# Modulation loads on ScalarE's DMA queue, and two early row loads at the first change of stage

## The chip, the cores and the metric

The kernel runs on one core of a Trainium2 chip. The metric is device time in microseconds, the median of three runs: 1107.7, from 1103.93 to 1109.38. The core has a matrix engine PE, the vector engine DVE, the scalar engine ACT and the general engine POOL; SP computes nothing here and issues DMAs. Each engine works through its own instructions in order. A DMA is issued by an instruction of one engine, runs on the core's 16 DMA engines, and raises a semaphore when it has landed.

## What is computed

One step of a two-layer model on 128 prompt tokens and 256 latent tokens (384 in all), width 1024, in float32. Layer 0 mixes tokens by a gated delta rule (8 heads, two directions, chunks of 64), layer 1 by windowed attention; each layer ends in a gated feed-forward part of width 2816.

```python
def modulation(cvec, w_ada, b_ada):              # w_ada: 1024 x 6144 per layer
    m = (silu(cvec) @ w_ada + b_ada)[:, None, :]
    return split(m, 6)                           # shift, scale, gate, twice

for i in range(2):
    mp, ms = modulation(c_ctx, ...), modulation(c, ...)
    h = rmsnorm(x, g0) * (1 + m[1]) + m[0]       # per stream, prompt and latent
    y = delta_mixer(h) if i == 0 else attention(h)
    x = x + m[2] * rmsnorm(y, g1)
    h = rmsnorm(x, g2) * (1 + m[4]) + m[3]
    f = (silu(a) * b) @ w_down                   # a, b: depthwise conv of h @ w_up
    x = x + m[5] * rmsnorm(f, g3)

# delta_mixer: per head and chunk solve (I + strict_lower(beta k k^T * decay)) u = rhs,
# then a scan over chunks carries the state S
```

The modulation weights w_ada are 48 MB for the two layers and are read whole, though each is used for two vectors only.

## The kernel before, in words

**Stages.** The kernel runs through layer 0's mixer (DeltaNet), a first feed-forward stage, attention and a second feed-forward stage. Each large product is split into a high and a low part of both factors, so three matmuls stand for one; ACT makes the high part of a weight (`whi`), DVE the low part (`wlo`), both from a raw 0.5 MB buffer (`raw`, three of them) that SP's queue fills. A stage ends in `tm` (L857): the output product, then per block of 128 tokens the squares on ACT (`stat`), `y<-bank,gate` on DVE (`t_gated`, L706), the update of `x`, squares again, `y<-x,arow` (`t_scale`), and diag matmuls on PE (`t_quarter`) that transpose y for the next stage, where its high and low parts are made (`hhi`, `hlo`). The last three products of each output bank (`tail`) are held back, so that PE has work while the first block goes through this. I call this a change of stage. `gate` and `arow` are rows of the modulation, read from DRAM (`gdram`, `adram`) and broadcast to 128 partitions by `t_rows` (L662), 1 MB each. At the first change of stage `tm` calls `hook` (L1142), which waits until all heads are done, takes a pool `dn3` in the memory that they leave, and loads `x` again (`x_prompt` 0.5 MB, `x_sample` 1 MB), because the DeltaNet stage uses x's memory as scratch.

**The modulation.** `t_ada` (L514) loads w_ada in slabs of 1 MB (128 x 2048): 40 of them through the slots `ada`, which are two buffers (`ada0`, `ada1`), and further one-use buffers that `lend` (L388) adds when some memory is free, among them the 1 MB buffers (`mem`) of heads 4 to 7 (L1411). `back` (L359) returns a slab's buffer. `t_mod` (L523) multiplies the slabs with silu(c) on PE (`bank<-ada,sc`), in 12 chunks per layer; a table `FILL` holds some chunks for the changes of stage.

**The inverse.** `t_inverse` (L1439) takes a head's matrix N through DRAM: it stores N (`nd<-N`), reads diagonal 16 x 16 blocks back (`tmp<-nd`, `X<-nd`), inverts them on POOL, stores the inverse's blocks (`zd<-inv`) and reads them in another layout (`x<-zd`; for the first heads the target is a part of x's memory). I call these transfers legs.

**The order of the work.** A list scheduler, `Sched` (L101), writes each engine's instructions. Tasks are generators that ask for an engine by a letter (P, A, V, G, and Q for SP's queue), for an event or for slots; of all tasks that wait, the one that could start first by the planner's costs is placed. `Sched.dma` (L136) costs a DMA at `DQ` = 0.47 us on Q, and at its bytes over `DBW` = 360 GB/s on one clock that all DMAs share. `Net.dma` (L322) issues all of them from SP:

```python
self.nc.sync.dma_start(out=out, in_=src)
```

The planner's costs only set the order. On the chip an instruction starts when the one before it on its engine and the semaphores it waits for let it. The DMAs' landings raise one of eight semaphores (`DMAHW0` to `DMAHW7` in the order's rows), and an instruction that issues a DMA can wait for one of them too.

Of the kernel before, what the change touches and what calls it, by code (L numbers as in the profile page):

```python
# [11 lines left out]
F32 = mybir.dt.float32  # L12
# [5 lines left out]
D = 1024  # L18
# [4 lines left out]
H = 8  # L23
# [27 lines left out]
DL1 = 0.25  # L51
DL2 = 1.6
DMIN = 0.06
DBW = 360.0
DQ = 0.47
SV = 0.0
ZD = 1
# [18 lines left out]
class Event:  # L76


    def __init__(self):
        self.time, self.waiters = None, []  # L80
# [20 lines left out]
class Sched:  # L101
# [5 lines left out]
    def __init__(self):  # L107
        self.free = dict.fromkeys("PAVGQ", 0.0)
        self.pending, self.runnable = [], deque()
        self.eng, self.start, self.cost, self.acts, self.bw, self.seq = None, 0.0, 0.0, [], 0.0, 0  # L110
        self.work = {}


# [5 lines left out]
    def set(self, ev):  # L119
        self.acts.append(lambda end: self._set(ev, end))  # L120

    def put(self, slots, *items):
        for i in items:
            self.acts.append(lambda end, i=i: self._put(slots, i, end))

    def use(self, letter, cost):
        assert letter == self.eng, (letter, self.eng)
# [7 lines left out]

    def dma(self, nbytes):  # L136

        self.use("Q", DQ)
        beg = max(self.start + self.cost + DL1, self.bw)
        self.bw = beg + max(DMIN, nbytes / (DBW * 1e3))  # L140
        ev = Event()
        ev.time = self.bw + DL2
        return ev


# [119 lines left out]
class Net:  # L265
# [55 lines left out]

    def dma(self, out, src):  # L322
        ev = self.s.dma(4 * math.prod(out.shape))
        self.nc.sync.dma_start(out=out, in_=src)  # L324
        return ev

    def load(self, out, src):
# [31 lines left out]
    def back(self, slots, item):  # L359

        if not any(item is o for o in self.once):
            self.s.put(slots, item)

    def free_bank(self, bank):

# [148 lines left out]
    def t_ada(self):  # L514
        for l, n, half in self.msrc:
            raw = yield self.ada, 1
            yield "Q"
            self.s.put(self.adaful, (raw, self.dma(raw, self.i["w_ada"][l, n, half])))

    def mod_prio(self):  # L520
# [336 lines left out]
    def tm(self, act, ready, plan, l, w, tail, nxt, hook=None):  # L857


        uses = {}  # L860
        for pieces in plan:
            for k, _ in pieces:
                uses[k] = uses.get(k, 0) + 1
        full = {k: Event() for k in uses}
        self.s.spawn(self.t_act(act, ready, plan, uses, full), 3)
        left = {hf: sum(h == hf for t in plan for _, h in t) for hf in range(2)}
        grid = lambda n: [[Event() for _ in range(n)] for _ in range(3)]
        ctx = dict(nxt=nxt, rg=grid(2), sq=grid(2), y=grid(2), sq2=grid(2), xa=grid(2), diag=[Event() for _ in range(3)], ready=[Event() for _ in range(3)])
        total = dict(left)
        acc = {}  # L870

        def piece(b, k, hf, wt, j, first, last):
            hi, lo = wt
            ah, al = full[k].val
            t, c = slice(b * 128, (b + 1) * 128), HALF[j]
            o = acc[hf][b]
            self.mm(o, ah[:, t], hi[:, c], start=first, stop=False)
            self.mm(o, ah[:, t], lo[:, c], start=False, stop=False)
            self.mm(o, al[:, t], hi[:, c], start=False, stop=last)

        held = []
        for n, pieces in enumerate(plan):
            if n == (len(plan) - tail if hook else 0):
                pool = hook() if hook else self.pool
                if hook:
                    pool = yield from pool
                ctx["gate"] = pool.tile([128, 2, D], F32, name="gate"), Event()
                self.s.spawn(self.t_rows(self.gates[l, w], self.gdram[l][w], *ctx["gate"]), 3)
                if nxt is not None:
                    ctx["arow"] = pool.tile([128, 2, D], F32, name="arow"), Event()  # L890
                    ctx["diags"] = [pool.tile([128, 128], F32, name=f"diag{b}") for b in range(3)]
                    ctx["shift"] = [pool.tile([128, n], F32R, name=f"shift{n}{m}") for m, n in enumerate((128, 128, 16))], Event()
                    self.s.spawn(self.t_shift(self.AB[nxt], *ctx["shift"]), 3)
                    self.s.spawn(self.t_rows(self.AB[nxt], self.adram[nxt[0]][nxt[1]], *ctx["arow"]), 3)
            wt = yield self.wready, 1
            for k, _ in pieces:
                yield full[k]
            if n >= len(plan) - tail:
                held.append((wt, pieces))
                continue  # L900
            for j, (k, hf) in enumerate(pieces):
                if hf not in acc:
                    acc[hf] = yield (self.bk if hf == 0 else self.pj), 3
                for b in range(3):
                    yield "P"
                    piece(b, k, hf, wt, j, left[hf] == total[hf], left[hf] == 1)
                left[hf] -= 1
                uses[k] -= 1
                if not uses[k] and k < self.recycle:
                    self.s.put(self.ahs, full[k].val)  # L910
            self.s.put(self.ws, wt)
        base = dict(left)
        if nxt is not None:
            self.boundary = Event()
        for hf in range(2):
            if not left[hf]:
                for b in range(3):
                    self.t_acc(b, hf, acc[hf][b], ctx)
        evs = []
        for b in range(3):  # L920
            for hf in range(2):
                for wt, pieces in held:
                    for j, (k, h) in enumerate(pieces):
                        if h == hf:
                            yield "P"
                            piece(b, k, hf, wt, j, False, left[hf] == 1)
                            left[hf] -= 1
                    if b == 2 and hf == max(h for _, h in pieces):
                        self.back(self.ws, wt)
                if base[hf]:  # L930
                    left[hf] = base[hf]
                    self.t_acc(b, hf, acc[hf][b], ctx)
            evs.append(self.s.spawn(self.t_block(b, ctx), 1 + b * 0.1))
        if nxt is not None:
            self.nearly = NE
            self.s.spawn(self.fm_first(NE, [([r[g] for r in ctx["rg"]], range(4 * g, 4 * g + 4), slice(0, NTOK)) for g in range(2)]), 10)
            self.s.set(self.fill[2 * l + w])
            evs.append(self.filled[2 * l + w])
        for e in evs:
            yield e  # L940
        if nxt is not None:
            self.s.set(self.boundary)
            self.boundary = None
# [150 lines left out]
    def delta(self, pool, nxt):  # L1094
        tc, i, s = self.tc, self.i, self.s
        with ExitStack() as late:
# [4 lines left out]
            t = lambda n, shape, dt=F32: hp.tile(shape, dt, name=n)  # L1101
# [12 lines left out]
                   for n in range(NB)]  # L1114
# [5 lines left out]
                                     R=t("R", [128, 2, 128]), sn=t("sn", [128, 2, 128]))])  # L1120
            self.norms = Slots([dict(osb=t(f"osb{n}", [128, 3, 128]), **{k: t(f"{k}{n}", [128, 3]) for k in ("so", "rt", "rs")})
                                for n in range(2)])
            self.odone = odone = [[Event()] for _ in range(H)]
            self.gateh, self.written = set(), set()
            s.spawn(self.t_zero(nqs, works), 8)
# [16 lines left out]
            def hook():  # L1142
                for e in chains + [o[0] for o in odone]:
                    yield e
                inner.close()
                pp = late.enter_context(tc.tile_pool(name="dn3", bufs=1))
                self.t512 = Slots([pp.tile([128, 512], F32, name=f"y{n}") for n in range(6)])
                wlast = self.pair(pp, "d")
                self.once.append(wlast)
                s.put(self.wlast, wlast)  # L1150
                yield "Q"
                self.load_x()
                return pp

            self.ahs, self.recycle = Slots(self.hslices()), 0
            plan = [[(2 * j, hf), (2 * j + 1, hf)] for hf, j in DN_OUT]
            yield from self.tm(self.oact, odone, plan, 0, 0, min(TAIL, 3), nxt, hook)

    def columns(self, m):
# [97 lines left out]
    def t_chain(self, h, t):  # L1257
        V, A, s = self.V, self.A, self.s
# [27 lines left out]
        N, Q, Y = nq["N"], nq["Q"], nq["Y"]  # L1286
# [106 lines left out]
        e = yield "AV" if h not in self.gateh else "V"  # L1393
# [13 lines left out]
        yield xc0  # L1407
        if h < H - 4:
            s.put(self.hslots, t)
        else:  # L1410
            self.lend(t["mem"].rearrange("p (j c) -> p j c", j=4))  # L1411

# [556 lines left out]
```

## Time and profile before

| what | value |
|---|---|
| median of three runs | 1107.7 us |
| profiled execution | 1107.74 us |
| its span | 1106.0 us |
| PE busy | 1062.2 us (96%) |
| PEld busy | 927.4 us |
| DVE busy | 696.2 us |
| ACT busy | 549.8 us |
| POOL busy | 235.0 us |
| mean granted clock of TensorE | 0.985 |
| bytes of the DMA queue | 176.61 MB |

PEld is PE's weight load, which runs beside matmuls. The clock is a share of full speed, so 1.00 is 2.4 GHz throughout. The span begins with the first instruction of the profiled execution; every "at so many us" counts from there. Of the views shown below, windows give the busy time of each engine in a stretch with the number of its instructions; the chain of waits has the start of a step, its length, and what it ran through; a timeline has the start, the length, engine, line, operation, output<-inputs, how many, and in brackets how long the engine was idle before and what released it. "SPq" is an issue of a DMA on SP's queue: its length is the issue's, not the transfer's.

### The profile page before, as it was taken

To read this page: it belongs to the slowest core of one execution; us is meant where nothing else is said; L and a number is where in the kernel's file an instruction comes from. 1 tells how busy PE (TensorE), PEld (TensorE's weight loads), DVE (VectorE), ACT (ScalarE), POOL (GpSimd) and SP (SyncE) were. 2 spreads that over 40 slices of the span, in tenths; PEclk is the share of its full clock that TensorE was granted. 3 is DMA by queue.
4 is the path that set the end of the run, shared out by engine and by line. 5 is a ranking of instruction groups with operands and counts; after the bars stand their busy time and mean duration, and the time that the engine had idled before them with its cause. 6 is when DMAs were issued, how large, how long until landed. Compare 5 with 4: busy or idle time off the path is not lost.

```text
span 1106.0 us, 19683 instructions
## 1 busy us (share of the span) xinstructions
PE 1062.2 (96%) x7397; PEld 927.4 (84%) x7397; DVE 696.2 (63%) x1685; ACT 549.8 (50%) x1127; POOL 235.0 (21%) x403
## 2 busy tenths in 40 slices
PE   6999899999998999999999999999999999999997
PEld 4887778899785999999988869776769999999886
DVE  5578656988546565656654456878577556566434
ACT  4576754767534444444543345566455444445422
POOL 0023545646202122222200021000031222221000
PEclk9999999999899999999999999998999999999999
DMA  9768664356345534533583346621514434335431
GB/s 364 279 224 293 189 193 127 104 167 204 96 166 223 199 126 132 196 120 128 169 316 126 113 133 220 212 95 41 192 35 142 132 118 132 126 123 172 129 119 57
DMA packets 73567, 177.86 MB, mean 161 GB/s; under 512 B 25816, under 2 KB 38744, under 8 KB 66432
## 3 DMA queue, kind: packets, MB, share of 16 engines
q1 hardware_dynamic: 73472, 176.61, 47.7%
q8 instruction: 58, 0.95, 0.3%
q14 instruction: 37, 0.30, 0.1%
HBM read 169.45 MB, written 7.13 MB: 160 GB/s over the span
## 4 chain that ended last, share of the span: by engine, by line
PE 81%; DMA 6%; DVE 5%; POOL 4%; issue 2%; ACT 1%; SPq 1%; DVEq 0%; POOLq 0%; ACTq 0%
PE bank L299 79%; PE bank L319 2%; POOL tmp L261 1%; DMA tmp<-nd 1%; DVE y L261 1%; POOL inv L261 1%; DMA gate<-gdram 1%; DMA nd<-N 1%; DMA x<-zd 1%; DMA ada<-in_w_ada 1%; DVE x L261 1%; DMA first<-in_w_ada 1%; SPq L324 1%; POOL stat L261 1%; DVE hlo L261 1%
## 5 line engine op out<-in xcount | busy, mean ns | idle before, releaser
L299 PE MATMUL bank<-hhi,whi 128*128 128x384 f32 x832 | 283.8, 341 | 4.1 <-DVE vf L261 2.8
L299 PE MATMUL bank<-hlo,whi 128*128 128x384 f32 x832 | 283.6, 341 | 0.2 <-DVE hlo L261 0.2
L299 PE MATMUL bank<-hhi,wlo 128*128 128x384 f32 x832 | 282.2, 339 | 0.0
L261 DVE TENSOR_TENSOR wlo<-raw,whi 128x1024 fp32r<-128x1024 f32 x151 | 184.9, 1225 | 64.1 <-ACT whi L261 64.0
L261 DVE SCALAR_TENSOR_TENSOR u<-bank,cw_ff,u 128x127 f32<-128x127 f32 x352 | 122.3, 410 | 145.3 <-ACT u L261 145.3
L261 ACT ACTIVATE whi<-raw 128x1024 fp32r<-128x1024 f32 x151 | 158.6, 1052 | 58.3 <-PE bank L299 46.8
L299 PEld LDWEIGHTS bank<-hhi,whi 128*128 128x128 f32 x832 | 156.7, 188 | 14.6 <-DVE vf L261 3.4
L299 PEld LDWEIGHTS bank<-hlo,whi 128*128 128x128 f32 x832 | 156.7, 188 | 4.2 <-issue 2.0
L299 PEld LDWEIGHTS bank<-hhi,wlo 128*128 128x128 f32 x832 | 156.7, 188 | 1.2 <-issue 0.8
L261 ACT ACTIVATE u<-bank,cw_ff 128x384 f32<-128x384 f32 x88 | 59.2, 673 | 177.2 <-PE bank L299 177.2
L261 POOL TENSOR_TENSOR g<-u 128x384 f32<-128x384 f32 x44 | 79.6, 1809 | 307.0 <-DVE u L261 276.6
L299 PE MATMUL bank<-whi,hhi 128*128 128x512 f32 (+1 forms) x246 | 96.7, 393 | 0.0
L299 PE MATMUL bank<-wlo,hhi 128*128 128x512 f32 (+1 forms) x246 | 94.1, 383 | 0.0
L299 PE MATMUL bank<-whi,hlo 128*128 128x512 f32 (+1 forms) x246 | 94.0, 382 | 0.0
L261 POOL TENSOR_TENSOR stat<-stat,mhalf 128x1 f32<-128x1 f32 x24 | 15.7, 656 | 253.0 <-DVE stat L261 253.0
L299 PE MATMUL bank<-hhi,wlol 128*128 128x384 f32 x200 | 67.9, 339 | 0.0
L299 PE MATMUL bank<-hlo,whil 128*128 128x384 f32 x200 | 67.7, 339 | 0.0
L299 PE MATMUL bank<-hhi,whil 128*128 128x384 f32 x200 | 67.7, 339 | 0.0
L261 DVE TENSOR_TENSOR wlol<-raw,whil 128x1024 fp32r<-128x1024 f32 x38 | 46.3, 1218 | 14.0 <-ACT whil L261 14.0
L299 PEld LDWEIGHTS bank<-whi,hhi 128*128 128x128 f32 x246 | 46.6, 190 | 9.6 <-issue 0.7
L299 PEld LDWEIGHTS bank<-whi,hlo 128*128 128x128 f32 x246 | 46.7, 190 | 9.2
L299 PEld LDWEIGHTS bank<-wlo,hhi 128*128 128x128 f32 x246 | 46.8, 190 | 8.0
(253 smaller groups left out, 1740.0 us busy)
## 6 DMA issues: line engine op xcount, KB each, us to landing
raw<-in_ffn_w_up SPq DMA_DIRECT2D x88, 512.0 KB
ada<-in_w_ada SPq DMA_DIRECT2D x32, 1024.0 KB
raw<-in_ffn_w_down SPq DMA_DIRECT2D x44, 512.0 KB
raw<-in_dn_w_in SPq DMA_DIRECT2D x29, 512.0 KB
first<-in_w_ada SPq DMA_DIRECT2D x6, 1024.0 KB
head<-in_w_ada SPq DMA_DIRECT2D x4, 1024.0 KB
raw<-in_dn_w_out SPq DMA_DIRECT2D x8, 512.0 KB
gate<-gdram SPq DMA_DIRECT2D x4, 1024.0 KB
```

What stands on the lines that cost most here:

```text
L261: return f(out, *a, **k)
L299: self.nc.tensor.matmul(out, lhsT, rhs, **kw)
L319: self.nc.tensor.transpose(out, src, ident)
L324: self.nc.sync.dma_start(out=out, in_=src)
```

## The change

Three things are changed. The modulation slabs of `t_ada` are issued from ACT (`yield "A"`), and the planner has a bandwidth clock of its own for each of the two queues (360 and 250 GB/s); a slab's buffer counts as free 2.0 us after its last use in the planner (`ADAGO`). At the first change of stage the rows gate and arow no longer get tiles of the pool dn3: the 1 MB buffers of heads 4 and 5, which were lent to slabs, receive them as soon as those heads are done (`lentrows`). And `hook` lends two more 1 MB tiles of dn3 (`adb0`, `adb1`) to slabs, after x's loads.

```diff
-DBW = 360.0
+DBWS = dict(Q=360.0, A=250.0)
+ADAGO = 2.0
@@ class Sched
-    def put(self, slots, *items):
+    def put(self, slots, *items, lag=0.0):
         for i in items:
-            self.acts.append(lambda end, i=i: self._put(slots, i, end))
+            self.acts.append(lambda end, i=i: self._put(slots, i, end + lag))
@@ def dma(self, nbytes):
-        self.use("Q", DQ)
-        beg = max(self.start + self.cost + DL1, self.bw)
-        self.bw = beg + max(DMIN, nbytes / (DBW * 1e3))
+        e = self.eng
+        self.use(e, DQ)
+        beg = max(self.start + self.cost + DL1, self.bw[e])
+        self.bw[e] = beg + max(DMIN, nbytes / (DBWS[e] * 1e3))
...
@@ class Net
-        self.nc.sync.dma_start(out=out, in_=src)
+        dict(Q=self.nc.sync, A=self.nc.scalar)[self.s.eng].dma_start(out=out, in_=src)
@@ def back(self, slots, item):
-            self.s.put(slots, item)
+            self.s.put(slots, item, lag=ADAGO if slots is self.ada else 0.0)
@@ def t_ada(self):
-            yield "Q"
+            yield "A"
@@ def tm
-                ctx["gate"] = pool.tile([128, 2, D], F32, name="gate"), Event()
-                self.s.spawn(self.t_rows(self.gates[l, w], self.gdram[l][w], *ctx["gate"]), 3)
+                if hook:
+                    ctx["gate"], ctx["arow"] = self.lentrows
+                else:
+                    ctx["gate"] = pool.tile([128, 2, D], F32, name="gate"), Event()
+                    self.s.spawn(self.t_rows(self.gates[l, w], self.gdram[l][w], *ctx["gate"]), 3)
...
@@ def hook
                 self.load_x()
+                self.lend(*[pp.tile([128, 4, 512], F32, name=f"adb{n}") for n in range(2)])
@@ def t_chain
         if h < H - 4:
             s.put(self.hslots, t)
+        elif h < H - 2:
+            rows, ev = t["mem"].rearrange("p (s d) -> p s d", s=2), Event()
+            self.lentrows.append((rows, ev))
+            s.spawn(self.t_rows(*((self.gates[0, 0], self.gdram[0][0]), (self.AB[0, 1], self.adram[0][1]))[len(self.lentrows) - 1], rows, ev), 3)
         else:
             self.lend(t["mem"].rearrange("p (j c) -> p j c", j=4))
```

**First place: SP's queue at the first head's inverse.** `nd0<-N0` is the leg out, `tmp<-nd0` and `X<-nd0` the leg back. Before:

```order
L324 DMA ada0_93<-in_w_ada 128x2048
L324 DMA ada1_94<-in_w_ada 128x2048
L324 DMA raw2_76<-in_dn_w_in 128x1024
L324 DMA nd0_627<-N0_624 128x6x128
L324 DMA mdram0_128<-modev0_95 4x512 x2
L324 DMA dm0_592<-gcdram_547 128x768
L324 DMA nd1_632<-N1_629 128x6x128
L324 DMA ada0_93<-in_w_ada 128x2048
L324 DMA tmp_641<-nd0_627 24x16x16
L324 DMA X_639<-nd0_627 24x16x16
```

The same place in the changed kernel:

```order
L327 DMA zd2_638<-Y2_636 128x192
L327 DMA raw0_74<-in_dn_w_in 128x1024
L327 DMA nd0_627<-N0_624 128x6x128
L327 DMA raw1_75<-in_dn_w_in 128x1024
L327 DMA tmp_641<-nd0_627 24x16x16
L327 DMA X_639<-nd0_627 24x16x16
L327 DMA raw2_76<-in_dn_w_in 128x1024
```

The three slabs are gone from SP's queue there, and a weight stands between the two legs in their place.

**Second place: ACT in the DeltaNet stage.** `vf1` and `head` are parts of a head, `modev` a chunk of modulation. ACT issues six slabs in its first 102 rows; here, at the tiles of head 7, come the next two in the changed kernel:

```order
L264 ACTIVATE vf1_591<-bank0_63,cw_dn_154 128x384
L264 ACTIVATE whi1_79<-raw0_74 128x1024
L264 COPY modev1_96<-bank3_66 128x512
L264 ACTIVATE junk_83,ss2_606<-bank5_68 128x128 x3
L327 DMA ada0_93<-in_w_ada 128x2048
L327 DMA ada1_94<-in_w_ada 128x2048
L264 ACTIVATE bank1_64<-bank1_64 128x384
```

In the kernel before no DMA stands on ACT; in the changed one none stands between its rows 102 and 230, and these are 230 and 231.

**Third place: the first change of stage.** SP's queue before, with `head2` a lent head buffer that takes a slab:

```order
L324 DMA raw2_76<-in_ffn_w_up 128x1024
L324 DMA raw0_74<-in_ffn_w_up 128x1024
L324 DMA head2_581<-in_w_ada 128x2048
L324 DMA x_71<-in_x_prompt 128x1024
L324 DMA x_71<-in_x_sample 128x2x1024
L324 DMA gate_3869<-gdram00_134 128x2048
L324 DMA arow_3870<-adram01_131 128x2048
L324 DMA raw1_75<-in_ffn_w_up 128x1024
```

In the changed kernel gate and arow are read further up in SP's queue, into `head4` (row 115) and `head0` (row 154); x's loads are rows 160 and 161. ACT at this place in the changed kernel, with what each instruction waits for (`DMAHW5` and `DMAHW6` are raised here by the loads of x_prompt and x_sample; `junk,stat00` are the squares of block 0):

```order
L264 COPY modev1_96<-bank4_67 128x512 [waits DMAHW4_49,PE_49]
L264 ACTIVATE whi2_81<-raw2_76 128x1024 [waits DMAHW3_49]
L327 DMA ada0_93<-in_w_ada 128x2048 [waits DMAHW7_49,DMAHW5_49]
L327 DMA ada1_94<-in_w_ada 128x2048 [waits DMAHW2_49]
L327 DMA adb0_3864<-in_w_ada 128x2048 [waits DMAHW5_49]
L327 DMA adb1_3865<-in_w_ada 128x2048 [waits DMAHW6_49]
L264 ACTIVATE junk_83,stat00_84<-bank6_69 128x512 [waits DVE_49]
L264 ACTIVATE junk_83,stat00_84<-bank2_65 128x512 [waits PE_49,Activation_49]
```

And PE there in the changed kernel, at block 0's diag matmuls:

```order
L302 MATMUL bank7_70<-wlod_3852,hhi_72 128x512
L302 MATMUL bank7_70<-whid_3851,hlo_73 128x512
L302 MATMUL bank3_66<-diag0_3866,y0_3845 128x128 x4
L302 MATMUL bank4_67<-diag0_3866,y1_3846 128x128 x4
L302 MATMUL bank6_69<-shift162_3871,shift1280_3869 128x512
L302 MATMUL bank6_69<-shift162_3871,shift1281_3870 128x512
L302 MATMUL bank5_68<-shift162_3871,shift1280_3869 128x512
L302 MATMUL bank5_68<-shift162_3871,shift1281_3870 128x512
L302 MATMUL bank7_70<-whid_3851,hhi_72 128x512
```

Four slabs stand on ACT ahead of block 0's squares where there were none. On PE the last nine matmuls of the tail (the last row is the first of them) now stand behind diag0; in the kernel before the whole tail and one slab's product stand ahead of it.

## Rows read from the trace of the kernel before

**Rows 1.** Windows: busy us (count) of PE, PEld, DVE, ACT, POOL; clock, DMA, GB/s

```profile
80.00:126.00 46.00, 40.47 (x244) 33.09 (x242) 34.50 (x102) 32.73 (x69) 16.25 (x44) 1.00 0.84 269
126.00:175.00 49.00, 46.20 (x683) 37.01 (x684) 28.65 (x85) 25.10 (x71) 26.08 (x80) 0.93 0.57 178
260.00:292.00 32.00, 30.01 (x405) 26.77 (x407) 22.25 (x60) 19.40 (x50) 15.20 (x43) 0.99 0.54 151
355.00:500.00 145.00, 145.00 (x852) 140.06 (x853) 86.73 (x173) 64.88 (x87) 28.70 (x16) 1.00 0.45 151
```

**Rows 2.** The chain of waits, first heads: start us, length us, what.

```profile
85.07 8.46 DMA nd<-N
93.59 6.01 DMA tmp<-nd
...
117.97 8.39 DMA x<-zd
...
148.85 9.47 DMA ada<-in_w_ada
...
164.96 6.18 DMA tmp<-nd
```

**Rows 3.** The chain of waits, one of the last heads.

```profile
265.46 2.87 DMA nd<-N
268.35 2.40 DMA tmp<-nd
...
286.96 2.73 DMA x<-zd
```

**Rows 4.** Timeline of SP's queue, 62 to 163 us, slabs: first, last.

```profile
62.95 0.35 SPq L324 DMA_DIRECT2D ada<-in_w_ada  x1
...
161.63 1.28 SPq L324 DMA_DIRECT2D ada<-in_w_ada  x2
```

**Rows 5.** Timeline of DVE at the first head's third leg.

```profile
126.39 0.38 DVE L261 STREAM_TRANSPOSE x<-x 128x192 f32<-128x192 f32 x1 [3.92 <-DMA x<-zd]
```

**Rows 6.** Timeline of SP's queue at the first change of stage.

```profile
323.11 0.38 SPq L324 DMA_DIRECT2D head<-in_w_ada  x1
...
324.02 0.78 SPq L324 DMA_DIRECT2D x<-in_x_sample  x1
```

**Rows 7.** The chain of waits at the first change of stage.

```profile
324.90 12.48 DMA gate<-gdram
```

**Rows 8.** Timelines of ACT and of DVE at the first change of stage.

```profile
327.54 0.60 ACT L261 ACTIVATE junk<-bank 128x512 bf16<-128x512 f32 x1 [1.59 <-PE bank L299]
...
337.41 1.29 DVE L261 TENSOR_TENSOR y<-bank,gate 128x512 f32<-128x512 f32 x2 [7.57 <-DMA gate<-gdram]
338.62 1.40 DVE L261 SCALAR_TENSOR_TENSOR x<-y,stat,x 128x512 f32<-128x512 f32 x2
```

**Rows 9.** Timeline of PE at the first change of stage.

```profile
337.32 0.39 PE L299 MATMUL bank<-wlo,hhi 128*128 128x512 f32 x1
337.55 0.39 PE L299 MATMUL bank<-whi,hlo 128*128 128x512 f32 x1
338.16 1.06 PE L299 MATMUL bank<-ada,sc 128*32 128x512 f32 x8 [0.23 <-DVE y L261]
343.21 3.48 PE L299 MATMUL bank<-diag,y 128*128 128x128 f32 x16 [3.98 <-DVE diag L261]
...
354.83 2.05 PE L299 MATMUL bank<-diag,y 128*128 128x128 f32 x16 [0.67 <-DVE diag L261]
```

**Rows 10.** The tile ada, its loads: least/median/most ns to issue; waits.

```profile
L324 SPq DMA_DIRECT2D ada<-in_w_ada x32: 327/340/1122, 10.9 to 705.9; - x32
```

**Rows 11.** Page, part 5: the power of the squares' sums on POOL.

```profile
L261 POOL TENSOR_TENSOR stat<-stat,mhalf 128x1 f32<-128x1 f32 x24 | 15.7, 656 | 253.0 <-DVE stat L261 253.0
```

**Rows 12.** Timeline of PE at the third change of stage.

```profile
807.66 2.05 PE L299 MATMUL bank<-diag,y 128*128 128x128 f32 x16 [0.16 <-DVE diag L261]
...
821.17 2.05 PE L299 MATMUL bank<-diag,y 128*128 128x128 f32 x16 [1.91 <-DVE diag L261]
```

More of the change, by code (lines that the diff above doesn't have):

```diff
@@ L109, in __init__ @@
         self.pending, self.runnable = [], deque()
-        self.eng, self.start, self.cost, self.acts, self.bw, self.seq = None, 0.0, 0.0, [], 0.0, 0
+        self.eng, self.start, self.cost, self.acts, self.seq = None, 0.0, 0.0, [], 0
+        self.bw = dict(Q=0.0, A=0.0)
         self.work = {}
@@ L136, in dma @@
     def dma(self, nbytes):
-        self.use("Q", DQ)
-        beg = max(self.start + self.cost + DL1, self.bw)
-        self.bw = beg + max(DMIN, nbytes / (DBW * 1e3))
+        e = self.eng
+        self.use(e, DQ)
+        beg = max(self.start + self.cost + DL1, self.bw[e])
+        self.bw[e] = beg + max(DMIN, nbytes / (DBWS[e] * 1e3))
         ev = Event()
-        ev.time = self.bw + DL2
+        ev.time = self.bw[e] + DL2
         return ev
@@ L886, in tm @@
                     pool = yield from pool
-                ctx["gate"] = pool.tile([128, 2, D], F32, name="gate"), Event()
-                self.s.spawn(self.t_rows(self.gates[l, w], self.gdram[l][w], *ctx["gate"]), 3)
+                if hook:
[3 more added lines that the diff above has]
+                    self.s.spawn(self.t_rows(self.gates[l, w], self.gdram[l][w], *ctx["gate"]), 3)
+                if nxt is not None and not hook:
+                    ctx["arow"] = pool.tile([128, 2, D], F32, name="arow"), Event()
+                    self.s.spawn(self.t_rows(self.AB[nxt], self.adram[nxt[0]][nxt[1]], *ctx["arow"]), 3)
                 if nxt is not None:
-                    ctx["arow"] = pool.tile([128, 2, D], F32, name="arow"), Event()
                     ctx["diags"] = [pool.tile([128, 128], F32, name=f"diag{b}") for b in range(3)]
@@ L893, in tm @@
                     self.s.spawn(self.t_shift(self.AB[nxt], *ctx["shift"]), 3)
-                    self.s.spawn(self.t_rows(self.AB[nxt], self.adram[nxt[0]][nxt[1]], *ctx["arow"]), 3)
             wt = yield self.wready, 1
@@ L1122, in delta @@
                                 for n in range(2)])
+            self.lentrows = []
             self.odone = odone = [[Event()] for _ in range(H)]
```

## The prediction, made before the changed kernel had run

> **What bounds the kernel now.** I read the busy time by stage first, then the chain of waits, then the timelines of the DMA-issuing SP queue, of PE and of DVE at the places where PE stood still. The stages show one bound: PE. From 355 to 500 us, in the first feed-forward stage, PE is busy 145.00 of 145.00 us [rows 1], and nothing that moves a load can help there. PE stands still before that, in the DeltaNet stage: 5.53 us of 46 between 80 and 126 us, 2.80 of 49 between 126 and 175, with a granted clock of 0.93 in the latter [rows 1]. The chain of waits says why: in those two stretches it runs through transfers, not through arithmetic. The matrix N of a head goes out to DRAM in 8.46 us and comes back in part in 6.01; the inverse's blocks come back in 8.39; a modulation slab holds PE's order for 9.47, and a later return takes 6.18 [rows 2]. The same three legs take 2.87, 2.40 and 2.73 us for one of the last heads [rows 3]. What differs is what stands ahead of them in SP's queue: between 62 and 163 us twelve 1 MB modulation slabs are issued there, in three places two at once just ahead of a leg [rows 4]. DVE, in order, stands 3.92 us behind the third leg [rows 5].
>
> The other still place is the first change of stage. Gate and arow are issued there behind a slab, x and two weights [rows 6]; gate lands 12.48 us later [rows 7], and DVE waits 7.57 us for it [rows 8]. PE then idles 3.98 us before the first diag matmul [rows 9].
>
> **The change part by part, made against the profiled execution: 1107.74 us, its span 1106.0 and 1.74 around it; the median of the three runs, 1107.7, is the same number.**
>
> *Slabs leave SP's queue.* Forty loads go to ACT, and the planner, whose costs changed, also puts them at other places. In the new order SP holds no slab around the first head's legs, and ACT holds four between the first heads and head 7's tiles where SP held twelve; the next stands behind head 7. So 8 MB leave the crowded stretch and come back after 225 us. Legs at the quiet price would be shorter by 8.46 - 2.87, 6.01 - 2.40, 8.39 - 2.73 and 6.18 - 2.40, and the wait of 9.47 would go: 28.1 us of the chain. That is not the gain, because PE works beside most of it. What PE can take back is its idle time, 5.53 + 2.80 = 8.3 us, less what a quiet stretch with the same small matmuls leaves idle, 32.00 - 30.01 = 2.0 [rows 1]: 6.3. The clock of 0.93 over 49 us is 3.4 us of PE's work lost after idling (1.2 instead of 2.4 GHz for part of it); I take 1 of it. Together 7.3. From below: nothing or a loss, if the eight slabs' matmuls, which filled holes, now leave holes and later stand in the way. From above: all 8.3 idle and 3.4 of clock, 11.7.
>
> *ACT issues.* An issue holds its queue 0.34 us by the median of the slabs' row [rows 10]; 40 are 13.6 us on ACT, whose work in the feed-forward stage is 64.88 of 145 us [rows 1]. That cover hides all but those inside a change of stage, two of the second: 0.7 us. Dearer is that ACT waits in order. A load can wait for the buffer's last reader, which the planner's 2 us are for, and also for the landing of another DMA that used the same completion semaphore before; 8 semaphores serve both queues. Behind it stand the conversions of weights and the evictions on which PE waits. No row of before has such a wait on ACT. Bounds: below 0.7, since most waited-for transfers stand far ahead in the order; above, for the thirteen loads between 225 and 320 us, four that hold ACT for a quiet leg of 2.4 us each [rows 3], with half of the 10 us reaching PE: 5. I take 0.7, the row of the issue.
>
> *Gate and arow early.* They land long before use, so DVE's 7.57 us end. What is late next is ACT. Its order there now has four slab loads ahead of block 0's two squares, and the third and fourth wait on the semaphores that x_prompt's and x_sample's loads raise (order, third place). So the squares start when x_sample has landed, though block 0 does not need it. In before the line ahead of gate's landing was half a weight's MB, a slab, 1.5 MB of x and gate itself, 4 MB in 12.48 us: 3.1 us a MB [rows 7]. x_sample therefore landed about 334.3, gate's MB earlier; without the slab it would be 331.2, and with the two slabs that ACT issues just before, sharing the engines, 334.3 again. From there: 0.5 of issues, two squares of some 0.75 [rows 8], y 0.65, the power on POOL with its neighbours about 1 [rows 11], then from the x update to the first diag matmul what before shows, 343.21 - 338.62 = 4.6 [rows 8, 9]: 8.2 us. In the new order PE stands at diag0 with nine matmuls of the tail behind it. In the third change of stage, where gate is resident and the order is that one, diag0 to the last diag takes 821.17 - 807.66 = 13.5 [rows 12]. The last diag comes at 331.2 + 21.7 = 352.9 or 334.3 + 21.7 = 356.0, against 354.83: a gain of 1.9 or a loss of 1.2. I take 0. From above: if PE found diag0 ready on arrival, nine matmuls of 0.23 before 337.93, the last would come at 335.9 + 13.5 = 349.4, a gain of 5.4.
>
> The early rows cost two 1 MB loads on SP in the DeltaNet stage's later part, in place of two of the four head slabs: nothing. Two more slab buffers (adb) are lent and read later. In the attention stage the order shifts by a few rows; I cost that at 0 with 2 either way.
>
> Sum: 1107.74 - 7.3 + 0.7 - 0 = 1101.1, so **1101 us**.
>
> Two rules of the Trainium skill bear on the first part, and they pull apart. Rows 2 and 3 show legs three times longer beside slabs in one queue; no row shows them with the slabs in another. "DMA: Bandwidth & Descriptors", section "Issuing engines are not separate DMA queues", says that DMAs from different issuing engines share the same engines and that only the sequencer's time is saved; by it alone the legs would not shorten wherever slabs still run, and the sum would be 1108.4. The same page, section "Queues, rings and completion order", says that an engine goes round between the queue rows packet by packet; by that a short transfer on SP's row would no longer wait for a slab's end, and all 11.7 us would come.
>
> **Rivals.** *B, the legs stay long or PE does not care.* The engines are 84% taken between 80 and 126 us [rows 1], and weights alone keep SP's line; holes then reopen where the eight slabs' matmuls stood. Against it: DVE and POOL wait for these legs by name. Gain of at most 1, cost 0.7: 1107. The first of the two rules would give this. *C, everything opens.* The legs fall to the quiet price, PE takes back 11.7, and the change of stage gains 1.9: 1107.74 - 13.6 + 0.7 = 1095. For it: 28.1 us of chain against 11.7 of PE; against: PE's order is fixed and small matmuls leave gaps of their own. The second rule would give this. *D, slower: ACT in order.* Loads that wait for a landing stop the conversions and evictions behind them. At the change of stage that is certain, and it loses once x_sample lands after 333.1 (354.83 - 21.7). If the slabs on ACT's queue make x_sample another 3.1 late, the loss is 4.3; with 5 in the late DeltaNet stage and no gain from the legs the time is 1117. It decides as soon as four such waits land on tiles PE has no others to run instead of. *E, the early rows do nothing*, because x is as late as gate was: that is my own value for that part, and lies in A and B.
>
> **How the numbers follow.** A, my forecast, 0.42, own range 1097 to 1104; B 0.25; C 0.18; D 0.15. Within 0.5% (5.5 us, about what a measurement of this kernel can tell from no change) means 1102.2 to 1113.2. Faster: 0.30 of A, all of C and 0.02 of B, 0.50. Slower: most of D, 0.14. Same: the rest, 0.36. For 8 in 10 the range leaves out the outer part of C and most of D: 1091 to 1113.
>
> **What would show it.** Right: in the chain, N's way out and back for the first heads at 3 to 5 us; PE idle under 5 us between 80 and 175; no DVE wait on gate at the first change of stage, but ACT waiting there for x's loads, with PE still 3 to 6 us at diag0. Wrong: legs above 6 us with no slab ahead on SP; PE's holes moved to 225 to 320 us; ACT waits on landings adding up to more than 5 us outside the change of stage; or block 0's squares starting before x_sample has landed.

## The result, and the profile after

The changed kernel takes 1133.79 us (median of 4 runs, 1131.88 to 1136.67) against 1106.40 us for the kernel before (median of 4): a ratio of 1.0249, 95% interval 1.0213 to 1.0284. It is 27 us slower, where 1101 us and a faster kernel were forecast.

PE's diag matmuls mark the ends of the stages in every kernel. In the timeline of PE of the changed kernel, the first and last diag of the first change of stage, the last of the second and the first of the third are these rows:

```profile
353.35 1.01 PE L302 MATMUL bank<-diag,y 128*128 128x128 f32 x3 [3.32 <-DVE diag L264]
...
368.50 0.71 PE L302 MATMUL bank<-diag,y 128*128 128x128 f32 x4 [1.74 <-DVE diag L264]
...
663.80 0.58 PE L302 MATMUL bank<-diag,y 128*128 128x128 f32 x1 [3.32 <-DVE diag L264]
...
830.21 1.05 PE L302 MATMUL bank<-diag,y 128*128 128x128 f32 x7 [0.16 <-DVE diag L264]
```

The last diag of the first change came at 354.83 before [rows 9] and comes at 368.50: 13.7 us are lost by then. The attention stage, from 663.80 to 830.21, takes 166.4 us against 157.5. Those are 22.6 of the 24.1 us by which the span grew (1106.0 to 1130.1); 1.6 more lie in the last stage.

The windows that answer to [rows 1], in the same columns:

```profile
80.00:126.00 46.00, 33.44 (x313) 29.38 (x314) 30.25 (x93) 26.98 (x67) 23.02 (x64) 0.78 0.55 167
126.00:175.00 49.00, 47.85 (x633) 43.44 (x632) 41.96 (x134) 36.31 (x102) 28.90 (x79) 1.00 0.38 95
```

The DMA engines are less busy, as forecast (0.55 for 0.84, 0.38 for 0.57). But PE stands still for 12.56 of 46 us where it was 5.53, and its granted clock there is 0.78: after the idle time it ran in part at the lower of its two levels. A hole also opened later, where PE had hardly idled before; the stretch from 175 to 260 us, before and after:

```profile
175.00:260.00 85.00, 84.27 (x1086) 74.45 (x1085) 72.77 (x227) 57.26 (x164) 50.33 (x133) 1.00 0.45 133
```

```profile
175.00:260.00 85.00, 79.54 (x855) 72.10 (x853) 62.38 (x180) 55.75 (x139) 28.33 (x74) 0.97 0.47 145
```

PE idles 5.46 us there where it idled 0.73. The chain of waits in the changed kernel, answering to [rows 2]:

```profile
84.81 4.38 DMA X<-nd
...
106.24 9.13 DMA tmp<-nd
...
131.86 3.14 DMA tmp<-nd
...
150.24 3.85 DMA x<-zd
...
247.46 3.24 DMA nd<-N
250.72 8.29 DMA tmp<-nd
```

Most legs are at 3 to 5 us, and the third leg of the first head is issued at 105.75 instead of 117.97. But two are as long as before. The timelines of ACT, SP, DVE and PE at the first of them (ACTq is an issue of a DMA by ACT):

```profile
105.74 0.39 ACTq L327 DMA_DIRECT2D ada<-in_w_ada  x1
...
106.22 0.39 ACTq L327 DMA_DIRECT2D ada<-in_w_ada  x1
```

```profile
105.75 0.38 SPq L327 DMA_DIRECT2D x<-zd  x1
106.24 0.47 SPq L327 DMA_DIRECT2D tmp<-nd  x1
```

```profile
115.22 0.38 DVE L264 STREAM_TRANSPOSE x<-x 128x192 f32<-128x192 f32 x1 [10.96 <-DMA x<-zd]
```

```profile
115.33 0.86 PE L302 MATMUL bank<-x,N 32*32 32x32 f32 x48 [8.15 <-DMA x<-zd]
```

ACT issues two slabs at the same moment as SP issues the two legs. The queues differ; the landing is as late as if the slabs stood ahead in one queue. DVE, in order, stands 10.96 us and PE 8.15. What the DMA engines did meanwhile, from 108 to 109 us (q10 is ACT's queue, q1 is SP's; packets, MB, share of the 16 engines' time):

```profile
q10 hardware_dynamic: 50, 0.41, 96.7%
q1 hardware_dynamic: 44, 0.01, 3.6%
```

The leg does not wait for the slabs' end: in this microsecond the two queues get about as many packets each. But the leg's packets are all under 0.5 KB and a slab's carry some 8 KB, so almost the whole time goes to the slabs.

DVE's waits for transfers between 25 and 325 us show the same as sums (us in total, times, longest). Before:

```profile
DVE x L261 <- DMA x<-zd: 9.4, 7, 3.9
...
DVE dm L261 <- DMA dm<-gcdram: 5.0, 2, 2.9
```

After:

```profile
DVE x L264 <- DMA x<-zd: 20.9, 7, 11.0
...
DVE dm L264 <- DMA dm<-gcdram: 6.9, 3, 5.3
```

14.4 us became 27.8, though fewer MB ran beside. At the first change of stage, ACT's timeline:

```profile
341.11 4.16 ACTq L327 DMA_DIRECT2D adb<-in_w_ada  x2
345.31 0.60 ACT L264 ACTIVATE junk<-bank 128x512 bf16<-128x512 f32 x1 [5.05 <-DMA x<-in_x_sample]
```

The squares of block 0 stand behind two adb loads that wait for x_sample's semaphore, as the prediction said. It is the only place where an issue holds ACT for long in this kernel: outside it no two issues together take more than 1.7 us. DVE no longer waits for gate.

### The profile page after: what moved, and what is told of

It is laid out like the page before. It is cut to its first block, busy times and chain, and to the rows that moved or that the text cites. A ratio compares the mean times of both kernels' runs of the same rounds, so it can differ in the third digit from the quotient of the medians.

```text
span 1130.1 us, 19658 instructions
## 1 busy us (share of the span) xinstructions
PE 1066.4 (94%) x7397; PEld 933.3 (83%) x7397; DVE 702.9 (62%) x1701; ACT 549.5 (49%) x1120; POOL 228.9 (20%) x396
## 4 chain that ended last, share of the span: by engine, by line
PE 75%; DMA 7%; POOL 6%; DVE 5%; issue 3%; ACT 2%; SPq 1%; POOLq 0%; DVEq 0%; ACTq 0%
PE bank L302 73%; POOL tmp L264 2%; POOL inv L264 2%; PE bank L322 2%; DMA tmp<-nd 2%; DMA dm<-gcdram 1%; DVE x L264 1%; DVE y L264 1%; SPq L327 1%; DMA zd<-inv 1%; DMA out_state_delta_new<-sn 1%; DMA first<-in_w_ada 1%; POOL stat L264 1%; DMA nd<-N 1%; DVE P L264 1%
## 5 line engine op out<-in xcount | busy, mean ns | idle before, releaser
L302 PEld LDWEIGHTS bank<-hhi,whi 128*128 128x128 f32 x832 | 158.0, 190 | 11.6 <-issue 3.6
```

Of the source, the lines that this page charges most:

```text
L302: self.nc.tensor.matmul(out, lhsT, rhs, **kw)
```

## The experiments

Times below are ratios to the kernel before on the same chip, with 95% intervals. The other columns are read from each kernel's PE timeline, in us: the first and the last diag of the first change of stage, and the attention stage from the last diag of the second change to the first of the third. Each of these columns is read from one execution, and the same order does not give the same number twice: the changed kernel and e14 have one order up to the first diag and differ by 2.8 us there, and the six kernels with PE's attention order of before (before, e1, e7, e8, e9, e14) take 155.9 to 157.6 us for that stage.

| kernel | ratio | first diag | last diag | attention |
|---|---|---|---|---|
| before | 1 | 343.21 | 354.83 | 157.5 |
| changed | 1.0249 (1.0213 to 1.0284) | 353.35 | 368.50 | 166.4 |
| e1, queue alone | 1.0068 (1.0046 to 1.0090) | 349.00 | 360.61 | 155.9 |
| e2, order alone | 1.0194 (1.0161 to 1.0227) | 351.02 | 365.62 | 166.5 |
| e3, early rows alone | 1.0012 (0.9995 to 1.0029) | 334.80 | 349.40 | 163.5 |
| e4, queue and costs | 1.0302 (1.0272 to 1.0332) | 369.48 | 382.01 | 161.6 |
| e5, one bandwidth clock | 1.0099 (1.0078 to 1.0121) | 341.77 | 358.35 | 160.0 |
| e6, no lag | 1.0221 (1.0184 to 1.0257) | 358.66 | 373.26 | 158.0 |
| e7, e3 with the old attention order | 0.9958 (0.9945 to 0.9972) | 333.99 | 348.60 | 155.9 |
| e8, before, new draw a | 0.9980 (0.9961 to 0.9999) | 338.40 | 350.68 | 157.6 |
| e9, before, new draw b | 1.0071 (1.0048 to 1.0093) | 348.62 | 360.61 | 157.4 |
| e10, four slabs on SP | 1.0209 (1.0189 to 1.0230) | 351.95 | 366.55 | 166.6 |
| e11, e7 with draw a | 1.0015 (0.9996 to 1.0034) | 342.87 | 357.46 | 154.9 |
| e12, changed, thin slabs | 1.0094 (1.0074 to 1.0114) | 341.03 | 355.63 | 168.5 |
| e13, before, thin slabs | 0.9905 (0.9884 to 0.9927) | 331.98 | 343.61 | 157.5 |
| e14, old plan after the first feed-forward | 1.0158 (1.0138 to 1.0177) | 356.13 | 371.32 | 157.6 |

**Queue and order apart.** The change does two things at once: it moves an issue to another queue, and it makes the planner write another order. e1 keeps the order of before on PE, DVE and POOL; e2 keeps that of the changed kernel, with the early rows and adb.

```diff
# e1, on before
-            self.s.put(self.adaful, (raw, self.dma(raw, self.i["w_ada"][l, n, half])))
+            self.s.put(self.adaful, (raw, self.dma(raw, self.i["w_ada"][l, n, half], self.nc.scalar)))
# e2, on after
-        dict(Q=self.nc.sync, A=self.nc.scalar)[self.s.eng].dma_start(out=out, in_=src)
+        self.nc.sync.dma_start(out=out, in_=src)
```

> The order of the kernel before, on every engine, with the 40 slabs issued from ACT at the planner's old places; rows as before. Theory O (the loss of 27 us comes from the new order of the work): about the time of before, 1103 to 1112, and the legs of the first heads stay above 6 us wherever slabs run beside them. Theory Q (the loss comes from ACT issuing and from its waits): 1125 to 1140. If the legs fall to 3 us and PE takes the time back, 1095 to 1101.

> The order of the changed kernel, early rows and adb included, with the slabs issued from SP. Theory O: about the changed kernel's time, 1126 to 1142. Theory Q: 1103 to 1112.

The order alone costs 1.94%, the queue alone 0.68%; the product of the two ratios, 1.0263, lies in the interval of the whole change. Theory O held for the larger part: e2's 1128.48 us lies in its range. e1's 1114.71 us lies between the ranges of O and Q, so the queue has a smaller part of its own. In e1 the chain of waits has the first legs at their old length, with slabs issued by ACT at 82.09 and 91.92 in flight beside them:

```profile
85.65 8.31 DMA nd<-N
94.03 5.90 DMA tmp<-nd
```

They were 8.46 and 6.01 with the slabs in SP's queue [rows 2]. And ACT's timeline in e1 shows what the queue costs:

```profile
162.72 6.47 ACTq L324 DMA_DIRECT2D ada<-in_w_ada  x2
169.23 0.32 ACT L261 COPY x<-bank 128x192 f32<-128x192 f32 x1 [5.99 <-DMA zd<-inv]
```

A slab has nothing to do with the inverse's blocks; its issue waits for the semaphore that zd<-inv raises (that landing is recorded at 168.78 us, and the second of the two issues starts at 168.80). The eviction behind it waits 5.99 us, and PE for that one; below, the same matmuls before:

```profile
169.60 0.91 PE L299 MATMUL bank<-Y,x 64*64 64x64 f32 x12 [4.49 <-ACT x L261]
```

```profile
161.85 0.57 PE L299 MATMUL bank<-Y,x 64*64 64x64 f32 x12
```

Just ahead of them PE is 3.5 us later than before, and with them 7.8 us: 4.3 of the 5.8 us that e1 has lost by the first diag arise here.

**The early rows.** e3 has the early rows and adb on the kernel before (slabs on SP, old costs); e4 is the changed kernel without them.

```diff
# e3, on before (e4, on after: these lines back to those of before)
+                if hook:
+                    ctx["gate"], ctx["arow"] = self.lentrows
...
+                self.lend(*[pp.tile([128, 4, 512], F32, name=f"adb{n}") for n in range(2)])
...
+        elif h < H - 2:
...
+            self.lentrows.append((rows, ev))
```

> The kernel before with the early rows of gate and arow and the two adb buffers alone; slabs from SP with the planner's old costs. Theory O: the order around the first change of stage and after it moves somewhat; 1098 to 1112. Theory R (the early rows, which take two slab buffers away, cost the time): 1120 to 1135.

> The changed kernel without the early rows and adb: slabs from ACT, planned with a bandwidth clock of their own and the lag of 2 us. Theory O: most of the loss stays, 1122 to 1138. Theory R: 1103 to 1112.

In e3 the last diag comes at 349.40, 5.4 us earlier, and the attention stage takes 6.0 us more. Before that stage PE's order differs from before's only around the change of stage; in the stage itself some 190 rows stand elsewhere (by PE's records; a moved row counts where it left and where it came). Theory R fell: without the rows (e4) the changed kernel is slower yet, 1139.35 us, which is just above O's range too.

**Is the attention stage's loss its order?** The planner's cost of a matmul depends on where it falls in windows of the planner's time, so the same work planned at another time can be ordered otherwise. e7 adds 1.9 us once to the planner's cost, which puts every row of PE's attention stage back:

```diff
# e7, on e3
+            self.shift = 1.9
             yield from self.ffn(0, (1, 0))
...
-        self.s.use("P", cost)
+        self.s.use("P", cost + self.shift)
+        self.shift = 0.0
```

> The early rows and adb alone, with 1.9 us added once to the planner's cost of a matmul at the start of the first feed-forward stage; no instruction is added, and PE's order in the attention stage is that of before again. Theory A (the 6.0 us that the rows-alone kernel lost in the attention stage are that stage's order and nothing else): the stage takes 157 to 158 us again, the first change of stage keeps its gain of 5.4, time 1101 to 1104. Rival (the two adb slabs, or what lands when, cost them): 163 us again, 1108.

> The changed kernel up to the first feed-forward stage; from there the old planner costs, slabs on SP, and 1.9 us added once to the planner's cost of a matmul, so that the attention stage has PE's order of before. If the attention stage's 8.9 us are its order: that stage takes 156 to 158 us and the whole 1120 to 1126. If they come from what the DeltaNet stage leaves: 164 to 167 us, 1130 to 1135.

e14 does the same for the changed kernel:

```diff
# e14, on after (with e7's two lines in the matmul's cost)
+            self.shift, self.s.shared = 1.90, True
             yield from self.ffn(0, (1, 0))
...
-            yield "A"
+            yield "Q" if self.s.shared else "A"
...
-            self.s.put(slots, item, lag=ADAGO if slots is self.ada else 0.0)
+            self.s.put(slots, item, lag=ADAGO if slots is self.ada and not self.s.shared else 0.0)
```

Windows over the whole attention stage, of before:

```profile
650.15:807.66 157.51, 152.74 (x1039) 121.59 (x1039) 111.31 (x367) 83.81 (x234) 10.86 (x15) 0.96 0.42 144
```

of the changed kernel:

```profile
663.80:830.21 166.41, 157.06 (x1047) 123.38 (x1048) 116.68 (x380) 79.05 (x221) 10.83 (x15) 0.94 0.40 142
```

and of e14:

```profile
666.61:824.23 157.62, 152.85 (x1040) 121.76 (x1040) 111.36 (x367) 83.87 (x234) 10.88 (x15) 0.96 0.41 145
```

The order explains all of the 8.9 us; e2, with the changed kernel's order and the slabs on SP, takes 166.5 too. About half of it is idle time (9.35 us of PE for 4.77). The other half is busy time: about 1 us is a slab's eight matmuls more, and the granted clock is 0.94 for 0.96. It does not take the new bandwidth clocks to get such an order: e3, planned with one bandwidth clock, takes 163.5, and e6 below, planned with two, takes 158.0. The place is the stage's end; in the changed kernel and, below, before:

```profile
794.00:830.21 36.21, 31.57 (x183) 23.55 (x182) 24.70 (x75) 15.61 (x48) 2.83 (x3) 0.91 0.24 88
```

```profile
780.00:807.66 27.66, 27.51 (x152) 21.57 (x152) 17.46 (x44) 12.66 (x33) 2.83 (x3) 1.00 0.53 186
```

Some heads' scores are left to the end, with no large matmul to fill their waits. e7, whose stage takes 155.9 us, is also the kernel that beats both: 1102.1 us, 0.42% under before. Its first and last diag of the first change of stage:

```profile
333.99 1.27 PE L300 MATMUL bank<-diag,y 128*128 128x128 f32 x9 [0.44 <-DVE diag L261]
...
348.60 0.60 PE L300 MATMUL bank<-diag,y 128*128 128x128 f32 x3 [1.73 <-DVE diag L261]
```

PE waits 0.44 us there where it waited 3.98 [rows 9], and has the tail's last nine matmuls behind diag0.

**Which of the planner's costs, and how much is the draw?** e5 counts both queues on one bandwidth clock of 360 GB/s; e6 takes the lag away. e8 and e9 change no cost: they add 1.8 and 3.2 us once, to the first matmul of the kernel before, and 913 and 1226 of PE's 1156 rows before the first diag are counted as moved (a moved row counts where it left and where it came).

```diff
# e5, on after
-        beg = max(self.start + self.cost + DL1, self.bw[e])
-        self.bw[e] = beg + max(DMIN, nbytes / (DBWS[e] * 1e3))
+        beg = max(self.start + self.cost + DL1, self.bw["Q"])
+        self.bw["Q"] = beg + max(DMIN, nbytes / (DBWS["Q"] * 1e3))
# e6, on after
-ADAGO = 2.0
+ADAGO = 0.0
# e8, on before (e9: 3.20), with e7's two lines in the matmul's cost
+        self.shift = 1.80
```

> The changed kernel, but the planner counts ACT's slabs and SP's transfers on one bandwidth clock of 360 GB/s again; slabs are still issued from ACT, buffers still with the lag of 2 us, rows early. Theory C (the separate clocks make the planner believe that a leg beside a slab is short, so that it puts DVE's and PE's instructions too early into their orders): DVE's waits for x<-zd and dm fall from 27.8 us towards 14, the first diag matmul comes at 340 to 346, time 1112 to 1122. Theory L (the order of before is one lucky draw among many, and any new one costs): no better than the changed kernel, 1122 to 1140.

> The changed kernel with the lag of 2 us for a slab's buffer set to 0; clocks still separate. If the lag starves PE of slabs to fill its holes, 1118 to 1128 and more slabs before 225 us; if the separate clocks are what costs, 1128 to 1142.

> The kernel before with 1.8 us added to the planner's cost of the first matmul, nothing else: 913 of PE's 1156 rows of the DeltaNet stage stand elsewhere, those of attention as before. Theory L: the first diag matmul comes 5 to 20 us later, 1113 to 1128. Theory C: a new order with the old costs is about as good, 1103 to 1111.

> The kernel before with 3.2 us added to the planner's cost of the first matmul, nothing else: 1226 rows of PE's DeltaNet stage are shifted, attention as before. Theory L: 1113 to 1128; theory C: 1103 to 1111.

One clock brings the first diag to 341.77 and DVE's waits to 15.0 us:

```profile
DVE x L264 <- DMA x<-zd: 8.0, 3, 4.0
...
DVE dm L264 <- DMA dm<-gcdram: 7.0, 5, 3.7
```

The lag is not what costs (e6, 1132.25 us). The two draws move the first diag by -4.8 and +5.4 us, of which the scatter of one order can be some 3, so one kernel proves little. But the three orders planned with separate clocks have it at 353.35 and 358.66 with the early rows (changed, e6) and 369.48 without (e4); the six with one clock at 334.80 to 342.87 with them (e3, e5, e11) and 338.40 to 348.62 without (before, e8, e9). DVE's waits for x<-zd and dm part the orders more clearly: 27.8 to 31.0 us in the three, 10.1 to 15.6 in the six. The most is in e6:

```profile
DVE x L264 <- DMA x<-zd: 25.2, 6, 11.2
...
DVE dm L264 <- DMA dm<-gcdram: 5.8, 2, 5.2
```

In the slower draw, e9, they are where before's are, though its first diag is late:

```profile
DVE x L261 <- DMA x<-zd: 11.2, 4, 6.7
...
DVE dm L261 <- DMA dm<-gcdram: 3.7, 3, 2.7
```

These waits go with the order and not with the queue. In e2, the changed kernel's order with slabs from SP, they are 26.6 us:

```profile
DVE x L264 <- DMA x<-zd: 15.2, 5, 5.0
...
DVE dm L264 <- DMA dm<-gcdram: 11.4, 4, 5.6
```

In e1, before's order with slabs from ACT, they are 12.2. Theory C has that for it in the DeltaNet stage; L is true on a smaller scale (e9's 1113.09 us lies in its range, e8's 1103.65 in C's). Of the six only e5 also plans the slabs on ACT, so it is the one close comparison with the changed kernel.

**Is it the slabs' traffic?** e12 and e13 load a sixteenth of each slab's columns, read sixteen times over, with the order of the changed kernel and of before.

```diff
-            self.s.put(self.adaful, (raw, self.dma(raw, self.i["w_ada"][l, n, half])))
+            self.s.put(self.adaful, (raw, self.dma(raw, self.i["w_ada"][l, n, half], 32)))
...
+        if thin:
+            out, src = out[:, :, :thin], src[:, :, :thin]
...
+                        self.mm(..., raw[:, j:j + 1, :32].to_broadcast([128, 16, 32]),
```

> The changed kernel, order and queues as they are, but of each slab only a sixteenth of the columns is loaded, and PE reads these sixteen times over: the modulation is computed from a part of the weights, and 37.5 MB less are moved. If the slabs' traffic beside the legs is what DVE and PE wait for: legs at 2 to 5 us everywhere, DVE's waits for x<-zd and dm under 15 us, first diag at 340 to 346, 1118 to 1126. If the new order waits in any case: DVE's waits above 20 us, 1128 to 1135.

> The kernel before, its order and its SP queue as they are, with a sixteenth of each slab loaded and read sixteen times over: the modulation is computed from a part of the weights. If the slabs' traffic costs the two orders alike, this gains the 16 us that the changed kernel gained, 1089 to 1094; if the old order had placed the slabs where they cost little, 1100 to 1106.

The traffic costs both orders nearly the same by the first diag, 12.3 and 11.2 us, so it isn't what sets them apart there: 9.0 of the 10.1 us remain without it. In the whole time the gains are less alike, 1.5% and 0.95% by the ratios (10.8 and 11.2 us between the spans of the profiled executions), and e13's 1096.83 us lies between its two ranges. DVE's waits in e12:

```profile
DVE x L264 <- DMA x<-zd: 15.9, 6, 7.3
...
DVE dm L264 <- DMA dm<-gcdram: 3.8, 2, 3.1
```

and in e13:

```profile
DVE x L261 <- DMA x<-zd: 2.3, 2, 1.6
...
DVE dm L261 <- DMA dm<-gcdram: 2.2, 1, 2.2
```

19.7 against 4.5 us with little slab traffic on the engines: in the new order DVE meets its instructions before their transfers have landed, even so. My expectation for e12 had these as alternatives; both were half right, and its 1117.85 us lies just under the first range.

**The squares behind x.** e10 issues the four slabs of the first change of stage from SP.

```diff
-            self.s.put(self.adaful, (raw, self.dma(raw, self.i["w_ada"][l, n, half])))
+            self.s.put(self.adaful, (raw, self.dma(raw, self.i["w_ada"][l, n, half], self.nc.sync if 16 <= k < 20 else None)))
```

> The changed kernel with the four slab loads of the first change of stage issued from SP instead of ACT; every other engine's order as it was. Theory D (ACT's squares wait 5 us behind these loads for x_sample's landing): no such wait, the first diag matmul 3 to 5 us earlier, 1128.5 to 1131.5. Rival (SP's later weights then stand behind slabs that wait for their buffers): what is gained there is lost after the change of stage, 1133 to 1136.

ACT's 5 us wait is gone and 1130.43 us lies in D's range, but the first diag comes only 1.4 us earlier and the last 1.95. But e10's execution was already 1.5 us behind where x is loaded, ahead of the place, as SP's queue shows in the changed kernel and, below, in e10:

```profile
336.00 0.38 SPq L327 DMA_DIRECT2D x<-in_x_sample  x1
```

```profile
337.50 0.38 SPq L327 DMA_DIRECT2D x<-in_x_sample  x1
```

From this issue on the first diag comes 2.9 us earlier and the last 3.5, the lower end of what was expected. e11 adds draw a to e7 (`self.shift = 1.8` at the start, and 1.8 again where e7 has 1.9).

> The early rows and adb with slabs on SP, the DeltaNet order of the planner shift by 1.8 us, and the attention order of before. If the gains add: DeltaNet 2 to 4 us and the rows 4 us against before, 1096 to 1101. If the two orders' gains are the same idle time: 1101 to 1106.

The gains didn't add: 1107.79 us lies above both ranges, and the first diag went to 342.87 from 333.99 in e7. Why is open. Up to 235 us every engine has e8's order in e11, and the first early row is issued at 244; but PE has lost most of what parts the two before that, going from 1.0 us ahead of e8 to 3.5 behind between 134 and 143 us. So most of that is not the rows' doing.

## Why the prediction was wrong, step by step

**Slabs leave SP's queue: -7.3 forecast.** This step failed. Its first half came: the DMA engines are less taken, and most legs are at 3 to 5 us. Its second half did not: PE was to take back 6.3 of its 8.3 us of idle time and 1 us of clock, but it idles 13.7 us between 80 and 175 (12.56 and 1.15), with a granted clock of 0.78 in the first of the two stretches and 1.00 in the second. The step counted the slabs that stand ahead of a leg in SP's queue [rows 4]. e1 shows that a slab costs a leg as much from ACT's queue, 8.31 and 5.90 us, and in the changed kernel two pairs on ACT fall on legs (105.74 and 248), which are as long as ever: the first of the signs named for being wrong, legs above 6 us with no slab ahead on SP. Of the Trainium skill's two rules on the page "DMA: Bandwidth & Descriptors", the one in the section "Issuing engines are not separate DMA queues" holds here (8.31 beside 8.46). The one in "Queues, rings and completion order" is seen too (44 packets of the leg beside 50 of the slabs in one microsecond), but not what I drew from it: taking turns did not let the leg past, since its packets are small. With nearly all slab traffic gone and the old order, the first diag came 11.2 us earlier (e13); that lies near my upper bound of 11.7, but it is all the slabs and not the eight that the change moves, so it is no test of the 7.3.

**What had no term: the new order itself.** I read from the order which slabs had gone, and priced the rest of the reordering at nothing in the DeltaNet stage and at 0 with 2 either way in attention. This is the larger failure. The attention stage's order did not shift by a few rows, as I read it: by PE's records some 580 rows stand elsewhere, counted where they left and where they came. The order alone was worth 1.94%, some 21 us (e2): 10.8 by the last diag of the first change, 9.0 in the attention stage (166.5 against 157.5).

**ACT issues: +0.7 forecast, bound 5.** Measured alone on before's order it is 0.68%, 7.5 us; between e2 and the changed kernel it is about 0.5%. In e1 the mechanism was the one named, a load that waits for the landing of another transfer on its semaphore, with an eviction behind it, and more than half of the loss by the first diag is one such wait; I took the nearest row, the length of an issue, where the upper bound was nearer. In the changed kernel none of the loads between 225 and 320 us waited so (nine by the trace, not thirteen), only the pair at 341.

**Early rows: 0 forecast.** Alone they bring the last diag from 354.83 to 349.40, the bound from above, 349.4. The way is the one of that bound: PE stood only 0.41 us at diag0 and had the nine matmuls behind it. That it fits to the tenth is luck: the first diag came at 334.80 for 335.9, the last 14.6 us after it for 13.5, and 1.7 of the 5.4 us were there by 298 us, ahead of the change of stage. In the changed kernel the forecast wait of the squares for x_sample was there (5.05 us) and cost about 3 (e10).

**The rivals.** B was right on the legs and wrong on the time. D gave the sign; its mechanism bears 6 to 7.5 us of 27, and the rest is a case I didn't have: a new order that the chip waits in. In the DeltaNet stage, some 10 us, the runs point to the planner's being told that the queues don't share (e5 and DVE's waits); in the attention stage, 9 us, they do not, since e3 has most of that loss with one bandwidth clock. C needed quiet legs, which only the kernels with thin slabs had (up to 4.3 us in their chains of waits).

What stays open: why the planner with separate bandwidth clocks puts these instructions so early was not followed instruction by instruction; that the clocks do it is shown by nine orders, with e5 as the one close comparison, and not by one isolated row. Why the attention order of the changed kernel and of e3 came out worse than the others was not followed either.

## What to carry to other kernels

Where a scheduler writes the order, separate the two halves of such a change first: run the new queue with the old order, and the new order with the old queue. Before pricing a reorder at zero, draw the order anew once or twice with a harmless shift; here that alone moved the time by -0.2% and +0.7%, so a gain below that can be the draw, and an order that suits can be kept while the rest is changed (e7). A queue of its own does not give a transfer bandwidth of its own, and a planner should not be told so.

## What was not expected of the hardware

A DMA issue on ACT held its engine 6 us for the landing of a transfer of another queue with which it shares nothing but the semaphore (6.47 us for two issues in e1, 4.16 for two in the changed kernel). And idle time can be paid twice: in the stretch where PE stood 12.56 us the granted clock was 0.78, and in e3's attention stage, with as many matmuls as before (1039), 1.6 us more idle came with 4.4 us more busy time and a granted clock of 0.94 for 0.96:

```profile
644.69:808.20 163.51, 157.12 (x1039) 123.56 (x1039) 114.36 (x374) 81.36 (x227) 10.87 (x15) 0.94 0.41 140
```

Nor did a queue of its own help the leg of small packets beside the slabs: from 108 to 109 us the engines gave it 44 packets for the slabs' 50, and with them 3.6% of their time.
